# The pooling gate by seven products, with twelve quarter loads a stage and the differences made earlier

## The chip, the cores and the metric

One core of one Trainium2 chip. The time is the device time of one execution in microseconds (us); lower is better. The kernel before takes 1189.01 us, the median of three runs (1187.78 to 1189.39).

## What is computed

One decoder block on a sequence of 1024 tokens of width 1024, all in float32. The parts that matter here:

```python
h = rms_norm(x, norm_gain) * (1 + scale) + shift
q, k, v, z_a, u, z_b, m_a, m_b = split(h @ w_in)
p_a = (attention(q, k, v) * silu(z_a)) @ w_branch_a
pooled = multiscale_causal_pool(u, pool_w, pool_scale)   # windows 2, 4, 8, 16
p_b = (pooled * silu(z_b)) @ w_branch_b
out = (sigmoid(m_a) * p_a + sigmoid(m_b) * p_b) @ w_out
return rms_norm(x + gate * out, final_gain)              # gate from silu(c) @ w_ada
```

For each channel the pool takes the mean of the last 2, 4, 8 or 16 tokens minus the token itself: this is a *difference* below. There are eight of them, d_0 to d_7, each 128 channels by 1024 tokens, with windows 2, 2, 4, 4, 8, 8, 16, 16.

## The kernel before

**Products.** A float32 operand is held as a high half (rounded to the fast format float32r) and a low half (what is left of it). A product is three: high by high, high by low, low by high. ScalarE (ACT) casts the high half, VectorE (DVE) subtracts the low half. TensorE (PE) multiplies 128x128 by 128x512.

**Stages.** In order of time: the normalised input `h` and the projection u; the values v; the gate m_b (*m* below); the gate z_b of the pooling branch; the branch product with `w_branch_b` (*b* below); attention together with the other projections; the output. The stages v, m and b each multiply 1024x1024 by 1024x1024, cut into four blocks of 512 a side, with seven block products instead of eight (`seven`, L576). They differ in what is multiplied (`b_of`), what is loaded (`load`) and what is done with the results (`final`: `values`, `gate_b` and `branch`).

**A set.** A block product, called p1 to p7, is a set of 48 matmuls of PE in two quarters of 24. For each quarter `a_op` (L557) makes an operand from weights, in the tag `whl` with two buffers, and `b_op` (L563) one from the input, where the block product wants a sum of input blocks (p5, p6, p7, p4; the sums of h are in `ht0` to `ht3`, made by `make_t` during u). p1, p2 and p3 of v and m read h itself. The sets run in the order p1, p5, p6, p7, p4, p3, p2. Weight blocks are loaded in quarters, 512 KB each, 18 loads a stage: blocks that are needed in several sums are loaded again. `s2k` holds a sum of weights that p6 and p3 share. The results of a set stand in four banks (columns) of PSUM; they are copied by ACT or added by DVE (`copied`, `added`) and then given to `final`.

**The gate stage.** For each of eight blocks of 128 channels the loop makes the difference (`load_u` from the stored u, `make_d`), runs a projection of 48 matmuls (`project`, line name wzb), takes silu on ACT, and multiplies by the difference and the scale on DVE (L739). Sums of these, `t1` and `t2`, are made for b (L743 to L746). Beside it a row of `w_gate` is loaded and multiplied by silu(c) with a running sum (L752), which gives the final gate.

**Order.** In these stages a scheduler orders each engine's instructions by priorities that follow the program's order; every engine then runs its own queue in order, and an instruction that waits holds up all behind it on its engine. `tc.keep_in_program_order` pins an instruction to its written place. Loads are issued by SyncE (SP) and, for the stores of u, by ACT. Tiles of pools that have been closed give their space to later pools, so a later tile's first writer waits for the last use of the earlier one.

Of the kernel before, what the change touches and what calls it, by code (L numbers as in the profile page):

```python
# [15 lines left out]
P = 128  # L16
D = 1024
# [34 lines left out]
def block_kernel(ctx, tc, a, out):  # L52
# [28 lines left out]
    u_d = dram.tile([KB, P, S], F32, name="u_d")  # L81

# [8 lines left out]
    const.tile([P, 24], F32, name="skip")  # L91
# [440 lines left out]
    dhls = {}  # L532

    def load_u(j):
        u = dif.tile([P, S + 16], F32, tag="u", bufs=2, name=f"u{j}")
        v.memset(u[:, S:], 0.0)
        nc.sync.dma_start(u[:, :S], u_d[j])
        return u

    def make_d(j, u):  # L540
        win = WINDOWS[j // 2]
        cur, n, step = u, S + 16, 1
        while step < win:
            nxt = dif.tile([P, S + 16], F32, tag="win", bufs=2, name=f"win{j}_{step}")
            n -= step
            v.tensor_add(nxt[:, :n], cur[:, :n], cur[:, step:step + n])
            cur, step = nxt, 2 * step
        t0 = S - win + 1
        d = dif.tile([P, S], F32, tag="d", bufs=5, name=f"d{j}")
# [4 lines left out]
        dhls[j] = d  # L554
# [21 lines left out]
    def seven(nm, sums, load, b_of, a_moves, ta, tb, final, direct):  # L576
# [3 lines left out]
        def raw(first, m, k, q, name):  # L580
            t = (wts if first else sums).tile([P, 2, 512], F32, tag="raw" if first else "ar", bufs=2, name=f"{nm}{name}_{q}")
            load(t, m, k, q)
            return t

        def a_s1(q):
            r, w = raw(1, 1, 0, q, "a21"), raw(0, 1, 1, q, "a22")
            v.tensor_add(r, r, w)
            w = raw(0, 0, 0, q, "a11s")
            v.tensor_sub(k2(s2k, q), r, w)
            return r  # L590

        def a_s3(q):
            r, w = raw(1, 0, 0, q, "a11d"), raw(0, 1, 0, q, "a21d")
            v.tensor_sub(r, r, w)
            return r

        def a_s4(q):
            r = raw(1, 0, 1, q, "a12s")
# [4 lines left out]
            p1=lambda q: raw(1, 0, 0, q, "a11"), p5=a_s1, p6=lambda q: k2(s2k, q), p7=a_s3,  # L603
            p4=lambda q: raw(1, 1, 1, q, "a22"), p3=a_s4, p2=lambda q: raw(1, 0, 1, q, "a12"),
# [8 lines left out]
        for name in ("p1", "p5", "p6", "p7", "p4", "p3", "p2"):  # L613
            c = {"p5": "b", "p3": "b", "p2": "c"}.get(name, "a")
            if c not in chain:
                chain[c] = [bank((tb if c == "b" else ta)[j // 2], f"{nm}{name}_{j}") for j in range(4)]
            ps = chain[c]
            for q in range(2):
                al, bl = a_op(a_of[name](q), f"{nm}{name}a{q}"), b_of(name, q)
                for j in range(4):  # L620
                    js = slice(j * P, j * P + P)
                    for e in range(2):
                        for i, (w, m) in enumerate(((0, 0), (0, 1), (1, 0))):
                            l, r = (bl(m, e)[:, js], al[:, w, e]) if a_moves else (al[:, w, e, js], bl(m, e))
                            mm(
                                ps[j], l, r, start=name in ("p1", "p5", "p2") and (q, e, i) == (0, 0, 0),
                                stop=(q, e, i) == (1, 1, 2), skip_group_check=True,
                            )
            for j in range(4):
                if name == "p1":  # L630
                    keep["s1", j] = copied("s1", 4, j, ps[j])
                elif name == "p6":
                    keep["s2", j] = copied("s2", 4, j, ps[j])
                elif name == "p7":
                    final(1, 1, j, added(copied("s3", 4, j, ps[j]), chain["b"][j]))
                elif name == "p4":
                    final(1, 0, j, ps[j] if direct else copied("s3", 4, j + 4, ps[j]))
                elif name == "p3":
                    final(0, 1, j, added(keep["s2", j], ps[j]))
                elif name == "p2":  # L640
                    final(0, 0, j, added(keep["s1", j], ps[j]))

    with ExitStack() as vps:
# [3 lines left out]
        tq = [vp.tile([P, 4, 512], F32, name=f"ht{i}") for i in range(4)]  # L647

# [4 lines left out]
        def difference(dst, x, y, name):  # L653
            tmp = vp.tile([P, 2, 512], F32, tag="tmp", bufs=1, name=name)
# [24 lines left out]
        early.close()  # L679

        vs = vps.enter_context(pool("vs", side="right"))

        def h_parts(nm):
            def of(name, q):
# [3 lines left out]
                return b_op(k2(tq[("p5", "p6", "p7", "p4").index(name)], q), vs, 2, f"{nm}{name}b{q}")  # L688
# [7 lines left out]
        def values(m, n, j, src):  # L696
            sb = 4 * n + j
            vo = vs.tile([P, 8, 2, HD], F32R, tag="vo", bufs=3, name=f"vo{sb}_{m}")
# [6 lines left out]
            )  # L705

        def gate_b(m, n, j, src):
            t = vs.tile([P, 512], F32, tag="go", bufs=3, name=f"sb{4 * m + j}_{n}")
# [3 lines left out]
        seven("v", vs, loads("w_v"), h_parts("v"), True, ("av", "tr"), ("pj", "z"), values, True)  # L712
        seven("m", vs, loads("w_mb"), h_parts("m"), False, ("pj", "z"), ("av", "tr"), gate_b, True)

    turns[0] = cycle(("av", "tr", "pj", "z"))
    diffs = ExitStack()
    dif = diffs.enter_context(pool("dif", side="right"))

    pbs = ExitStack()
    pb = pbs.enter_context(pool("pb"))  # L720
    gb = pb.tile([P, KB, S], F32, name="gb")
    t1 = pb.tile([P, 4, 512], F32, name="t1")
    t2 = pb.tile([P, 4, 512], F32, name="t2")
# [499 lines left out]
```

## Time and profile before

| what | us |
|---|---|
| median of three runs | 1189.01 |
| the profiled execution | 1187.59 |
| its span, first to last instruction | 1185.8 |
| PE busy | 1169.2 |
| stage v | 128.5 to 204.6 |
| stage m | 204.6 to 280.8 |
| gate stage | 280.8 to 367.8 |
| stage b | 367.8 to 444.5 |

The granted TensorE clock is 0.998 of full speed in the mean. In the rows below, PE is TensorE, DVE VectorE, ACT ScalarE, POOL GpSimd, SP SyncE; a q behind the name is the engine's queue of DMAs. A row of a view by time has start, duration, engine, line, operation, output<-input, size and, in brackets, how long the engine was idle before it and what ended that. A row of groups has total busy time and mean nanoseconds, then idle time ahead. A row by tile has min/median/max nanoseconds and the first and last start. A row of DMA issues has the count, the size and the median time from issue to landing.

### The profile page before, as it was taken

How to read it: one execution, taken by the hardware profiler on the slowest of the kernel's cores; microseconds unless marked ns; L12 is line 12 of the kernel's file. 1: busy time of each engine (PE TensorE's matmuls, PEld its weight loads, DVE VectorE, ACT ScalarE, POOL GpSimd, SP SyncE). 2: the span in 40 equal slices, each digit the busy share in tenths (PEclk: the TensorE clock that was granted, in tenths of full speed). 3: DMA queues.
4: the chain of work that ended last, by engine and by line, in shares of the span. 5: the costliest groups of instructions: out<-in, count | busy, mean ns of one | idle time of the engine just before them, and what ended most of it. 6: DMA issues, size and time to landing. Idle time of an engine off the chain costs nothing.

```text
span 1185.8 us, 15373 instructions
## 1 busy us (share of the span) xinstructions
PE 1169.2 (99%) x5602; PEld 975.0 (82%) x5602; DVE 832.4 (70%) x1072; ACT 588.3 (50%) x1137; POOL 216.7 (18%) x248
## 2 busy tenths in 40 slices
PE   8999999999999999999999999999999999999997
PEld 7888888888888887888888888887888888888876
DVE  5767467555996651878788788879787973894653
ACT  5561355454313532667666666666666764232111
POOL 1000000000000004124234242443343622000001
PEclk9999999999999999999999999999999999999999
DMA  9651529546535257322333142423333126984622
GB/s 349 257 193 62 180 103 318 187 162 234 200 103 176 97 179 222 79 81 91 84 98 90 62 121 54 135 62 103 94 88 99 37 72 208 349 280 157 213 70 73
DMA packets 74750, 172.49 MB, mean 145 GB/s; under 512 B 9393, under 2 KB 22833, under 8 KB 72498
## 3 DMA queue, kind: packets, MB, share of 16 engines
q1 hardware_dynamic: 68770, 160.82, 41.6%
q10 hardware_dynamic: 5904, 10.68, 2.5%
q8 instruction: 44, 0.72, 0.3%
q14 instruction: 32, 0.26, 0.1%
HBM read 121.14 MB, written 33.56 MB: 130 GB/s over the span
## 4 chain that ended last, share of the span: by engine, by line
PE 84%; DVE 7%; DMA 3%; issue 3%; ACT 2%; SPq 0%; POOL 0%; POOLq 0%; DVEq 0%; ACTq 0%
PE p L101 24%; PE wzb L101 7%; PE mp L101 6%; PE vp L101 6%; PE bp L101 6%; PE o L101 6%; PE pa L101 5%; PE u L101 5%; PE z L101 5%; PE av L101 4%; PE wt L101 4%; PE ua L101 3%; DVE om L942 2%; DVE be L101 2%; PE wm L101 1%
## 5 line engine op out<-in xcount | busy, mean ns | idle before, releaser
L101 PE MATMUL p<-hT,w 128*128 128x512 f32 x1536 | 392.7, 392 | 1.3 <-DVE klo L101 1.3
L101 PEld LDWEIGHTS p<-hT,w 128*128 128x128 f32 x1536 | 283.0, 188 | 59.5 <-DVE klo L101 1.7
L942 DVE TENSOR_TENSOR_SCAN om<-om,eye 128x511 f32<-128x511 f32 (+7 forms) x128 | 184.0, 1442 | 68.9 <-ACT om L938 68.3
L149 POOL TENSOR_TENSOR w<-w_raw,w 128x256 fp32r<-128x256 f32 x124 | 124.8, 1037 | 571.5 <-ACT w L146 571.5
L938 ACT ACTIVATE om<-z 128x512 f32<-128x512 f32 (+2 forms) x192 | 95.0, 495 | 109.2 <-PE z L101 46.8
L962 DVE TENSOR_TENSOR wt<-wt,wt 128x512 fp32r<-128x512 f32 (+1 forms) x160 | 99.0, 619 | 15.7 <-ACT wt L961 14.7
L101 PE MATMUL av<-wt,vv 128*128 128x512 f32 x320 | 106.0, 412 | 0.1
L961 ACT CAST wt<-wt 128x512 fp32r<-128x512 f32 (+1 forms) x160 | 88.2, 551 | 35.0 <-PE wt L101 34.8
L101 DVE TENSOR_TENSOR be<-be,om 128x512 f32<-128x512 f32 (+7 forms) x128 | 98.5, 775 | 0.0
L101 PE MATMUL wt<-ident,be 128*128 128x128 f32 x576 | 90.3, 274 | 3.9 <-DVE wt L962 3.1
L939 ACT ACTIVATE be<-z 128x512 f32<-128x512 f32 (+2 forms) x192 | 94.0, 489 | 0.0
L101 PE MATMUL pa<-ga,wa 128*128 128x512 f32 x384 | 89.9, 390 | 0.9 <-DVE s L1115 0.8
L101 PE MATMUL o<-wo,mhl 128*128 128x512 f32 (+1 forms) x408 | 89.6, 377 | 0.0
L101 PE MATMUL wzb<-hT,wzb 128*128 128x512 f32 x384 | 87.2, 389 | 0.0
L101 PEld LDWEIGHTS pa<-ga,wa 128*128 128x128 f32 x384 | 71.9, 188 | 16.5 <-issue 1.2
L101 PEld LDWEIGHTS o<-wo,mhl 128*128 128x128 f32 x408 | 73.5, 188 | 14.1
L101 PEld LDWEIGHTS wt<-ident,be 128*128 128x128 f32 x576 | 69.5, 140 | 18.7 <-DVE wt L962 6.2
L101 PEld LDWEIGHTS wzb<-hT,wzb 128*128 128x128 f32 x384 | 72.1, 188 | 15.0
L991 POOL TENSOR_TENSOR tp<-tp,tl 128x256 f32<-128x256 f32 x32 | 38.1, 1190 | 153.9 <-DVE tp L988 153.9
L101 PE MATMUL z<-kl,q 128*128 128x512 f32 (+2 forms) x192 | 65.5, 341 | 0.0
L101 PE MATMUL z<-kh,q 128*128 128x512 f32 (+2 forms) x192 | 64.1, 334 | 0.0
L101 PE MATMUL u<-hT,wg 128*128 128x512 f32 x240 | 55.5, 391 | 0.0
(265 smaller groups left out, 1650.0 us busy)
## 6 DMA issues: line engine op xcount, KB each, us to landing
w_raw<-in_w_in SPq DMA_DIRECT2D x32, 512.0 KB, 3.5
v_d<-vo SPq DMA_DIRECT2D x16, 512.0 KB, 4.2
vv<-v_d SPq DMA_DIRECT2D x8, 1024.0 KB, 6.3
wa_raw<-in_w_branch_a SPq DMA_DIRECT2D x16, 512.0 KB, 4.7
wa<-in_w_mod SPq DMA_DIRECT2D x7, 1024.0 KB, 7.4
kh<-kh SPq DMA_DIRECT2D x48, 128.0 KB, 2.3
va<-in_w_v SPq DMA_DIRECT2D x10, 512.0 KB, 4.0
ma<-in_w_mb SPq DMA_DIRECT2D x10, 512.0 KB, 4.4
```

The lines of the kernel that those rows point to most:

```text
L101: ins = op(*args, **kw)
L149: gp.tensor_tensor(hl[:, 1, es], raw[:, es], hl[:, 0, es].bitcast(F32), op=ALU.subtract)
L938: act.activation(om[:, 1 + b0:1 + b0 + n], zp[:, :n], AF.Sigmoid, scale=-0.125)
L939: act.activation(be[:, b0:b0 + n], zp[:, :n], AF.Sigmoid, scale=0.125)
L942: v.tensor_tensor_scan(om[:, 1:W], om[:, 1:W], eye[:, :W - 1], 0.0, ALU.mult, ALU.max)
L961: act.copy(wt[:, 0, :off], pt[:, :off])
L962: v.tensor_sub(wt[:, 1, :off], pt[:, :off], wt[:, 0, :off].bitcast(F32))
L991: gp.tensor_add(tp, tp, tl)
```

## The change

The gate stage becomes a fourth `seven`, named z, in place of eight projections: 336 matmuls instead of 384. Its results go to `gate_z`, which loads the stored difference (`ds`, three buffers) for each column. All four stages get the new form of `seven`: the sets run in the order p1, p2, p6, p7, p5, p4, p3; block 11 of the weights is kept in tiles of its own (`a11`, in the new pool `vb`) and block 22 too, so that a stage makes 12 quarter loads instead of 18; in each quarter the high by high products of the first three columns (two in the second quarter) come first, and then the rest, column by column.

The differences are made during v and m: `paced` gives, for each set, what is done behind it ("load" j begins the load of u_j or of a row, "use" j makes the difference or multiplies the row; a name with "-" is done ahead of the set's results). They are stored in DRAM (`d_d`) and loaded again in z. The loads are begun by GpSimd's queue: `begin` lets GpSimd read one column of a result that has just been made (the mark), and issues the DMA behind it. The rows of `w_gate` go the same way in z and b. The first VectorE operation of each use is pinned.

```diff
+    def begin(dst, src, mark):
+        gp.tensor_scalar(spare[:, :1], mark[:, :1], 1.0, 0.0, op0=ALU.mult, op1=ALU.add)
+        tc.keep_in_program_order(gp.dma_start(dst, src))
...
-        nc.sync.dma_start(u[:, :S], u_d[j])
+        begin(u[:, :S], u_d[j], mark)
...
-            v.tensor_add(nxt[:, :n], cur[:, :n], cur[:, step:step + n])
+            ins = v.tensor_add(nxt[:, :n], cur[:, :n], cur[:, step:step + n])
+            if step == 1:
+                tc.keep_in_program_order(ins)
...
-        dhls[j] = d
+        gp.dma_start(d_d[j], d)
...
+        def a_s2(q):
+            r = raw("raw", 1, 0, q, "a21")
+            v.tensor_sub(a11[q], a11[q], r)
+            a22[q] = raw("a22", 1, 1, q, "a22")
+            v.tensor_sub(k2(s2k, q), a22[q], a11[q])
+            return k2(s2k, q)
...
-        for name in ("p1", "p5", "p6", "p7", "p4", "p3", "p2"):
+        for name in ("p1", "p2", "p6", "p7", "p5", "p4", "p3"):
...
+                ahead = 3 - q
+                parts_ = [(j, e, 0, 0) for j in range(ahead) for e in range(2)]
                 for j in range(4):
+                    for e in range(2):
+                        parts_ += [(j, e, w, m) for w, m in ((0, 0), (0, 1), (1, 0))[j < ahead:]]
...
-                return b_op(k2(tq[("p5", "p6", "p7", "p4").index(name)], q), vs, 2, f"{nm}{name}b{q}")
+                return b_op(k2(tq[("p5", "p6", "p7", "p4").index(name)], q), vb, 2, f"{nm}{name}b{q}")
...
-            nc.sync.dma_start(sb_d[4 * m + j][:, 512 * n:512 * n + 512], t)
+            act.dma_start(sb_d[4 * m + j][:, 512 * n:512 * n + 512], t)
...
+        pooled = paced(load_u, make_d, (
+            ("v", "p2", [("load", 3)]), ("v", "p6", [("use", 3), ("load", 0)]), ("v", "p7", [("load", 2)]), ("v", "p5-", [("use", 0)]),
+            ("v", "p5", [("load", 1)]), ("v", "p4", [("use", 2), ("load", 5)]), ("v", "p3", [("use", 1), ("load", 7)]),
+            ("m", "p1", [("use", 5), ("load", 6)]), ("m", "p6", [("use", 7), ("load", 4)]), ("m", "p5-", [("use", 6)]), ("m", "p4", [("use", 4)]),
+        ))
...
+        def modulated(j, wg_):
+            tc.keep_in_program_order(
+                v.scalar_tensor_tensor(wg_, wg_, 1.0, sg, ALU.mult, ALU.mult, accum_out=gate[:, j:j + 1]))
...
+            def gate_z(m, n, j, src):
+                ct = 4 * m + j
+                ds = zg.tile([P, 512], F32, tag="ds", bufs=3, name=f"ds{ct}_{n}")
+                gp.dma_start(ds, d_d[ct][:, 512 * n:512 * n + 512])
+                z = gq[m, n][:, j]
+                act.activation(z, src, AF.Silu)
+                v.scalar_tensor_tensor(z, ds, psc_v[:, ct:ct + 1], z, ALU.mult, ALU.mult)
+                return z
...
         def load_v(p):
-            nc.sync.dma_start(pair[p]["vv"].rearrange("p b h i d -> p (b h i d)").bitcast(F32), v_d[p].rearrange("p b c -> p (b c)"))
+            tc.keep_in_program_order(
+                nc.sync.dma_start(pair[p]["vv"].rearrange("p b h i d -> p (b h i d)").bitcast(F32), v_d[p].rearrange("p b c -> p (b c)")))
```

In b, the sums of the gated values are no longer made ahead: `g_parts` makes them on VectorE when p6, p5 and p4 ask for them, in `ht3` (for t1), `t2` and, for p5, in the block itself.

The change moves instructions in each queue. Three places follow. In a row, a name is the tile, with what it is read from behind the arrow; the brackets name the semaphores that it waits for (a name that ends in HW is a DMA of SP or ACT, in SW one of GpSimd).

**ACT, from the end of u to p1 of v.** `u0_sg1` is the last piece of u on its way to DRAM; `vp5b`, `vp6b` are b operands and `vp1a` weights of v. Before, with p1's weights cast long ahead:

```order
L185 COPY u0_sg1_1079<-u0_1_1054 128x512 [waits DMAHW2_49,PE_49]
L186 DMA u_d_78<-u0_sg1_1079 128x512 [waits Activation_49]
L565 CAST vp5b0_1174<-ht0_832 128x1024 [waits DVE_49]
L565 CAST vp5b1_1212<-ht0_832 128x1024 [waits DVE_49]
L609 COPY vs1_0_1151<-vp1_0_1089 128x512 [waits PE_49]
```

And after:

```order
L186 COPY u0_sg1_1083<-u0_1_1058 128x512 [waits DMAHW1_49,PE_49]
L187 DMA u_d_78<-u0_sg1_1083 128x512 [waits Activation_49]
L571 CAST vp6b0_1270<-ht1_834 128x1024 [waits DVE_49]
L571 CAST vp6b1_1306<-ht1_834 128x1024 [waits DMAHW3_49,DMAHW2_49,DVE_49]
L565 CAST vp1a0_1111<-va11_0_1109 128x1024 [waits DMAHW4_49]
L565 CAST vp1a1_1140<-va11_1_1138 128x1024 [waits DMAHW5_49]
L565 CAST vp2a0_1181<-va12_0_1179 128x1024 [waits DVE_49,PE_49]
```

The casts of p1's weights have moved behind the last piece of u and behind two casts for p6, of which the second waits for two DMAs: the last two stores of u, whose space its tile takes.

**VectorE in v, behind p2's results.** `vo2`, `vo3` are values on their way out, `win` and `d3` belong to difference 3, `vp7a`, `vp7b` are p7's operands. After:

```order
L733 TENSOR_TENSOR vo3_0_1253<-vs13_3_1173,vo3_0_1253 128x8x64 [waits Activation_49]
L550 TENSOR_TENSOR win3_1_1341<-u3_1257 128x1039 [waits DMASW0_49]
L566 TENSOR_TENSOR vp7a0_1355<-va11_0_1109,vp7a0_1355 128x1024 [waits Activation_49]
L550 TENSOR_TENSOR win3_2_1343<-win3_1_1341 128x1037 [waits DVE_49]
L572 TENSOR_TENSOR vp7b0_1358<-ht2_835,vp7b0_1358 128x1024 [waits Activation_49]
L556 SCALAR_TENSOR_TENSOR d3_1345<-win3_2_1343,u3_1257 128x1021 [waits DVE_49]
```

Before, no difference was made in this stage; p7's low halves followed p6's:

```order
L566 TENSOR_TENSOR vp6b1_1272<-ht1_833,vp6b1_1272 128x1024 [waits Activation_49]
L560 TENSOR_TENSOR vp7a0_1312<-va11d_0_1307,vp7a0_1312 128x1024 [waits Activation_49]
L566 TENSOR_TENSOR vp7b0_1315<-ht2_834,vp7b0_1315 128x1024 [waits Activation_49]
L560 TENSOR_TENSOR vp7a1_1347<-va11d_1_1342,vp7a1_1347 128x1024 [waits PE_49,Activation_49]
L566 TENSOR_TENSOR vp7b1_1350<-ht2_834,vp7b1_1350 128x1024 [waits Activation_49]
```

What is new there is the first window addition, which waits for a DMA of GpSimd and has p7's low halves behind it.

**ACT in b, at p5's second quarter.** `bs13` are copies of p7's results, `bp5a`, `bp4a` weights, `bp5b`, `bp4b` b operands. After:

```order
L620 COPY bs13_7_3192<-bp1_3_2886 128x512 [waits DMAHW4_49,PE_49,Pool_49]
L565 CAST bp5a1_3238<-ba11s_1_3235 128x1024 [waits DVE_49,Activation_49]
L565 CAST bp4a0_3278<-ba22_0_3041 128x1024 [waits PE_49,Activation_49]
L571 CAST bp5b1_3242<-ht2_835 128x1024 [waits DVE_49]
L571 CAST bp4b0_3282<-t2_2881 128x1024 [waits DVE_49,Activation_49]
```

Before, at the same product:

```order
L565 CAST p5b1_2955<-t1_2199 128x1024 [waits PE_49]
L559 CAST bp5a0_2914<-ba21_0_2906 128x1024 [waits DVE_49,Activation_49]
L609 COPY bs1_0_2894<-bp1_0_2826 128x512 [waits DMAHW5_49,DMAHW7_49,DMAHW2_49,PE_49]
L609 COPY bs1_1_2896<-bp1_1_2827 128x512 [waits PE_49]
L609 COPY bs1_2_2898<-bp1_2_2828 128x512 [waits PE_49]
L609 COPY bs1_3_2900<-bp1_3_2829 128x512 [waits PE_49]
L559 CAST bp5a1_2952<-ba21_1_2944 128x1024 [waits DVE_49,Activation_49]
```

The cast of p5's second b operand stood ahead of its first quarter's weights; now it stands behind the cast of p4's first weights, which waits for PE: that tile takes the buffer of p5's first quarter's weights. Its low half stands, on VectorE, behind these:

```order
L566 TENSOR_TENSOR bp5a1_3238<-ba11s_1_3235,bp5a1_3238 128x1024 [waits PE_49,Activation_49]
L824 TENSOR_TENSOR ht2_835<-ht2_835,g00_2310 128x1024
L566 TENSOR_TENSOR bp4a0_3278<-ba22_0_3041,bp4a0_3278 128x1024 [waits Activation_49]
L826 TENSOR_TENSOR t2_2881<-ht1_834,t2_2881 128x1024
L611 TENSOR_TENSOR ba12s_1_3389<-ba12s_1_3389,bs2k_2882 128x1024 [waits DMAHW6_49,DVE_49]
L572 TENSOR_TENSOR bp5b1_3242<-ht2_835,bp5b1_3242 128x1024 [waits Activation_49]
```

Here p4's low half, p4's difference and p3's weights are ahead of it.

More of the change, by code (lines that the diff above doesn't have):

```diff
@@ new lines, in seven @@
+                ends = {j: i for i, (j, *_) in enumerate(parts_)}
+                begun = set()
+                for i, (j, e, w, m) in enumerate(parts_):
+                    js = slice(j * P, j * P + P)
+                    l, r = (bl(m, e)[:, js], al[:, w, e]) if a_moves else (al[:, w, e, js], bl(m, e))
+                    mm(
+                        ps[j], l, r, start=name in ("p1", "p5", "p2") and q == 0 and j not in begun,
+                        stop=q == 1 and ends[j] == i, skip_group_check=True,
+                    )
+                    begun.add(j)
@@ L638, in seven @@
                 elif name == "p3":
[L639 to L641 removed]
+                    mark = final(0, 1, j, added(keep["s2", j], ps[j]))
+            for do in beside.get(name, ()):
+                do(mark)
     with ExitStack() as vps:
@@ L713, in block_kernel @@
[L713 to L723, printed above, removed]
-    gate = pb.tile([P, KB], F32, name="gate")
-    bias = pb.tile([P, KB], F32, name="gbias")
@@ L774, in branch, with paced, first_, then @@
-    def branch(m, n, j, t):
-        nc.sync.dma_start(pb_d[4 * m + j][:, 512 * n:512 * n + 512], t)
-    seven("b", sums, load_b_w, g_parts, False, ("av", "tr"), ("pj", "z"), branch, False)
-    pbs.close()
+            act.dma_start(sb_d[4 * m + j][:, 512 * n:512 * n + 512], t)
+            return t
+        banks = ("av", "tr"), ("pj", "z")
+        def paced(load, use, where):
+            held, todo = {}, {}
+            def first_(j, mark):
+                held[j] = load(j, mark)
+            def then(j, mark):
+                use(j, held.pop(j))
+            for stage, name, js in where:
+                todo.setdefault((stage, name), []).extend(
+                    [(lambda mark, j=j: first_(j, mark)) if at_ == "load" else (lambda mark, j=j: then(j, mark)) for at_, j in js])
+            return lambda stage: {name: dos for (st, name), dos in todo.items() if st == stage}
@@ new lines, in block_kernel @@
+        pooled = paced(load_u, make_d, (
[3 rows of a table added]
+        ))
+        seven("v", vs, loads("w_v"), h_parts("v"), True, *banks, values, True, pooled("v"))
+        seven("m", vs, loads("w_mb"), h_parts("m"), False, *banks, gate_b, True, pooled("m"))
+        diffs.close()
+        gp_ = vps.enter_context(pool("gp_", side="right"))
+        gate = gp_.tile([P, KB], F32, name="gate")
+        bias = gp_.tile([P, KB], F32, name="gbias")
+        nc.sync.dma_start(bias, a["b_gate"])
+        act.activation(sg, sg, AF.Silu)
@@ new lines, in block_kernel @@
+        with pool("zg", side="right") as zg:
+            def gate_z(m, n, j, src):
[6 more added lines that the diff above has]
+                return z
+            seven("z", vs, loads("w_zb"), h_parts("z"), False, *banks, gate_z, True, rows("z"))
```

148 lines of the change are left out of this document (73 added, 75 removed), and 4 rows, old and new, of the table rows.

## The prediction

> **What bounds the kernel now.** I read the page's busy shares, its chain, then busy time by stretches of the span and the stages' groups.
>
> ```profile
> PE 1169.2 (99%) x5602; PEld 975.0 (82%) x5602; DVE 832.4 (70%) x1072; ACT 588.3 (50%) x1137; POOL 216.7 (18%) x248
> PE   8999999999999999999999999999999999999997
> PE 84%; DVE 7%; DMA 3%; issue 3%; ACT 2%; SPq 0%; POOL 0%; POOLq 0%; DVEq 0%; ACTq 0%
> core 0: us, PE busy (x) PEld busy (x) DVE busy (x) ACT busy (x) POOL busy (x), PEclk, DMA share, GB/s
> 128.50:204.60 76.10, 76.10 (x337) 63.03 (x336) 51.30 (x55) 38.02 (x50) 0.00 (x0) 1.00 0.64 217
> 204.60:280.80 76.20, 76.20 (x338) 63.08 (x337) 43.30 (x44) 36.30 (x49) 0.00 (x0) 1.00 0.53 180
> 280.80:367.80 87.00, 87.00 (x385) 72.06 (x384) 73.17 (x107) 22.91 (x31) 0.00 (x0) 1.00 0.52 170
> 367.80:444.50 76.70, 76.70 (x336) 62.92 (x335) 49.20 (x48) 34.78 (x43) 2.84 (x4) 1.00 0.45 155
> 444.50:480.00 35.50, 34.24 (x151) 28.03 (x150) 8.20 (x9) 11.37 (x20) 13.13 (x19) 1.00 0.67 199
> ```
>
> PE is busy for 99% of the span and never idle in the four stages v, m, gate, b (76.1, 76.2, 87.0, 76.7 us of themselves); the clock is 1.00. So a removed product is worth its full pitch, and any operand that is late costs its full lateness: there is no slack on PE to lose it in. VectorE has room in v, m and b (51.3, 43.3, 49.2 us busy) and little in the gate stage (73.2 of 87.0).
>
> **What the change removes.**
>
> ```profile
> L101 PE MATMUL wzb<-hT,wzb x384: 389/389/389, 281.0 to 367.8; 128*128 128x512 f32 x192
> L101 PE MATMUL vp<-vp1a,hT x48: 389/389/389, 128.7 to 139.3; 128*128 128x512 f32 x48
> L609 ACT COPY bs<-bp 128x512 f32<-128x512 f32 x16 | 9.4, 587 | 6.9 <-PE bp L101 6.9
> ```
>
> 384 products start over 86.8 us: 0.2266 us each. Seven sets of 48 are 336, so 48 go: **−10.9 us**. Nothing else leaves PE. A set takes 48 × 0.2266 = 10.9 us, a quarter 5.4, and a quarter's first pass of hi·hi products covers 6 products (1.36 us) in a set's first quarter, 4 (0.91 us) in its second. That is the time for which a low half may lag its high half without cost.
>
> **Where VectorE's work goes.**
>
> ```profile
> L546 DVE TENSOR_TENSOR win<-u 128x1039 f32<-128x1039 f32 x8 | 9.9, 1235 | 5.5 <-DMA u<-u_d 5.5
> L752 DVE SCALAR_TENSOR_TENSOR wg<-wg,sg 128x1024 f32<-128x1024 f32 x8 | 9.8, 1221 | 0.6 <-DMA wg<-in_w_gate 0.5
> L739 DVE SCALAR_TENSOR_TENSOR gb<-d,vecs,gb 128x512 f32<-128x512 f32 x16 | 11.9, 746 | 7.5 <-ACT gb L738 7.5
> L550 DVE SCALAR_TENSOR_TENSOR d<-win,u 128x1021 f32<-128x1021 f32 x2 | 2.4, 1222 | 0.0
> ```
>
> Differences 3, 0, 2, 1 are made in v: 6 window additions of 1.235 and 4 scalings of 1.222, 12.3 us, so 51.3 becomes 64 of 76. Differences 5, 7, 6, 4 in m: 14 additions and 4 scalings, 22.2 us, 43.3 becomes 66. The new gate stage is m's 43.3, 16 scalings (11.9) and four modulation rows (4.9): 60. b gets six more 1024-wide subtractions (7.3) and four rows (4.9): 61. Every stage fits, so the sum is not bound by VectorE's total; it is bound by the order in which its work stands, since a pinned operation that waits holds up the low halves behind it. I walked the four stages along the new order with these durations.
>
> **The start of v.**
>
> ```profile
> 128.69 5.60 PE L101 MATMUL vp<-vp1a,hT 128*128 128x512 f32 x24
> 128.89 0.59 ACT L185 COPY u_sg<-u 128x512 f32<-128x512 f32 x1 [4.85 <-PE u L101]
> 129.50 0.33 ACTq L186 DMA_DIRECT2D u_d<-u_sg  x1
> L559 ACT CAST vp1a<-va x2: 1052/1054/1055, 71.2 to 81.4; 128x1024 fp32r<-128x1024 f32 x2
> u_d<-u_sg ACTq DMA_DIRECT2D x16, 256.0 KB, 2.0
> ```
>
> Before, p1's weights were cast at 71 and 81 us, so PE went on at once. After, ACT's queue has ahead of them two casts for p6, and the second waits for the landing of the last two stores of u, because its tile takes their space. The last copy starts at 128.89 as now, its store is issued at 129.50 and lands 2.0 later, 131.5; then two casts of 1.05 (or 0.96 at their pitch) and signals: PE restarts at about 133.8. **+5.1 us.** The low half follows one subtraction later, inside the 1.36 us of cover. For less, the store would have to land sooner; the bounds are 4.5 and 6.5.
>
> **v, behind p6.**
>
> ```profile
> u<-u_d SPq DMA_DIRECT2D x8, 512.0 KB, 4.7
> x<-in_x SPq DMA_DIRECT2D x8, 512.0 KB, 6.5
> wa<-in_w_mod SPq DMA_DIRECT2D x2, 512.0 KB, 10.0
> L235 POOL TENSOR_TENSOR st<-st,mhalf x8: 547/554/899, 12.5 to 67.1; 128x1 f32<-128x1 f32 x8
> ```
>
> u3's load begins after the last cast of p2's values (a GpSimd operation first, near 0.55 us by the nearest row), and its window addition is the first thing on VectorE ahead of p7's low halves. From that cast to p7's seventh product, window addition, low half, second addition and low half take 4.7 us, which leaves the load 3.7 us from mark to landing of the 8 to 9 that lie between that cast and p7's seventh product. No row shows a load on GpSimd's queue. The same load on SP took 4.7, and 512 KB took between 3.5 and 10.0 here: 4.7 stalls PE by 1.0, 6.5 by 2.7, 10.0 by 6. I take 5.5, since the mark adds to SP's 4.7: **+1.8 us**, ends 0 and 6.
>
> The row bounds this load from SP's side only. The Trainium skill, "DMA: Bandwidth & Descriptors", section "Anatomy of one DMA — SWDGE (gpsimd) path", fits 2.0 us plus bytes over 436e3 for a GpSimd DMA, an estimate of 3.2 us here, by which this term would be 0 and the sum 1.8 lower; no run here shows it.
>
> **m, gate and b.**
>
> ```profile
> ma12s<-in_w_mb SPq DMA_DIRECT2D x2, 512.0 KB, 4.4
> wg<-in_w_gate SPq DMA_DIRECT2D x8, 512.0 KB, 4.0
> 205.65 1.22 DVE L587 TENSOR_TENSOR ma<-ma,ma 128x1024 f32<-128x1024 f32 x1
> 206.78 0.68 DVE L573 TENSOR_TENSOR vs<-vp,vs 128x512 f32<-128x512 f32 x1
> 380.02 1.06 ACT L559 CAST bp5a<-ba 128x1024 fp32r<-128x1024 f32 x1 [0.19 <-DVE ba L587]
> 380.98 1.04 ACT L565 CAST p6b<-t 128x1024 fp32r<-128x1024 f32 x1
> ```
>
> Back to back, a 1024-wide subtraction takes 1.13 us and a cast 0.96. In m, p6's first low half ends about 1.3 us into p6 at best; behind it stand two additions and the scaling of difference 7, a sum of p2 (0.6) and the second quarter's operand with its low half: 1.3 + 0.6 + 5 × 1.13 = 7.6, due at 5.4 + 0.9 = 6.3. That is 1.3 late, and difference 5's row ahead adds about half an operation: **+1.9** (ends 1.3 and 3.3). Ahead of p4's low halves stand in m three additions of difference 6 and a subtraction that waits for a12's load (4.4 us), in the gate stage such a subtraction and a modulation row (4.0 on SP): each most of one operation late, **+0.9** and **+0.9** (ends 0 and 2). In b, p7 waits 0.4 behind row 4 (ends 0 and 2). **b's p5 is the second firm stall**: in ACT's queue the cast of p4's weights stands ahead of the cast of p5's second b operand, and it waits until PE has left p5's first quarter, whose weight tile it takes. So two casts (2 × 0.96, with signals 2.2) run after the quarter's end before PE can go on. It then has 0.91 us of hi·hi products, and the low half they lead to is the fourth of a row on VectorE that starts when p4's cast is done: p4's low half, p4's difference, p3's weights, p5's low half, 4 × 1.13 behind 1.1, ready 5.7 after the quarter's end. 5.7 − 0.91: **+4.8** (ends 2.2, the casts alone, and 6). p4 itself then finds its operands ready.
>
> **Start of attention.**
>
> ```profile
> 444.89 2.36 SPq L848 DMA_DIRECT2D vv<-v_d  x2
> 447.35 0.38 SPq L775 DMA_DIRECT2D pb_d<-bs  x1
> 455.96 1.07 ACT L833 CAST kh<-p 128x512 fp32r<-128x512 f32 x2 [9.64 <-DMA pb_d<-bs]
> 457.32 1.89 PE L101 MATMUL p<-hT,w 128*128 128x512 f32 x7 [1.26 <-DVE klo L101]
> ```
>
> The last store of b is stuck behind two loads of values, kh's cast waits for it, and PE idles 1.26. The loads move behind it: **−1.3**, ends 0 and −1.3. What follows has the same instructions on PE.
>
> **The sum**: −10.9 − 1.3 + 5.1 + 1.8 + 1.9 + 0.9 + 0.9 + 0.4 + 4.8 = +3.6 on the profiled execution's 1187.6 (its span 1185.8), and so on the median, 1189.0: **1192.6**. New work that I cost at nothing: GpSimd's marks and stores of differences (POOL is idle there), and the extra copies on ACT (0.59 each, half idle). If ACT had no slack beneath them, each copy would show with its 0.59.
>
> **Rivals.** *B, VectorE is never late.* What ACT's queue makes late is lost (start of v, and the two casts at b's p5), but loads land within 3.7 us and the hi·hi products cover the low halves: −10.9 − 1.3 + 5.1 + 2.2 = −4.9, **1184.1**, faster. It decides at 2.5 us: if VectorE's lateness, 8.5 us by my walk (1.8, 1.9, 0.9, 0.9, 0.4 and 2.6 of p5), stays under that in all, the change wins by over 0.2%. For it: five of the six terms are of a size that a load landing 2 us sooner removes. Against: the row ahead of p5's low half stands in the order itself.
> *C, loads on GpSimd's queue land late.* At 8 us for a load, v's p7 costs 2.5 more, m's p6 2, rows in the gate stage and b's p7 3, and gate_z, with four loads on three buffers, 2 to 3: **1202**. For it: 10.0 us for 512 KB occurs in this trace. Against: v's DMA share is 0.64, m's 0.53.
> The Trainium skill, "SBUF — State Buffer", section "SBUF: two separate sides", says that GpSimd writes the descriptors of its own DMAs and is locked out while VectorE runs a two-port copy, so such loads can starve; by that C is what happens where VectorE is busiest, but VectorE's operations in these stages are two-input ones and scalings, and no run here shows it.
> *D, the change does all that it says.* No stall shows, as ACT's casts and stores turn out not to hold each other: 1189.0 − 12.2 = **1177**. Against: both waits stand in the order.
>
> **How the numbers follow.** My sum, 1188 to 1197: 0.46 (0.17 of it under 1191.4). B, 1183 to 1188: 0.24 (0.15 of it under 1186.6). C, 1197 to 1206: 0.22. D: 0.08. A measurement of this kernel can tell about 0.2%, 2.4 us, from no change. So faster 0.15 + 0.08 = 0.23; same 0.17 + 0.09 = 0.26; slower 0.29 + 0.22 = 0.51. The range 1184 to 1202 leaves out D, the tail of C and little of B, under 0.2.
>
> **What would show it.** PE idle some 5 us before vp1's first product, named by ACT's cast behind the landing of u's stores; in b some 5 us lost at p5's second quarter; PE idle before p7 of v with VectorE's window addition waiting for u; the gate stage 10.9 us shorter in PE busy; no wait for klo at attention's start. The prediction is wrong if v starts without a gap, if p5's second quarter follows at once, or if loads on GpSimd land far from 5.5 us.

## The result, and the profile after

The changed kernel takes **1203.6 us**, the median of four runs (1202.49 to 1206.14), beside 1188.58 (1187.78 to 1189.39) for the kernel before on the same chip: a ratio of 1.0129, with a 95% interval of 1.0110 to 1.0149. It is slower by 15.0 us. The forecast was slower by 3.6, with 1202 as the upper end: the sign was right, the size was not, and the time lies 1.6 us above the range.

The page's busy shares of the changed kernel, its PE slices with the granted clock, and its chain:

```profile
PE 1163.9 (97%) x5554; PEld 967.2 (81%) x5554; DVE 862.1 (72%) x1100; ACT 613.0 (51%) x1165; POOL 253.4 (21%) x305
PE   8999899999999988999999999999999999999997
PEclk9999899999999999999999999999999999999999
PE 77%; DVE 10%; DMA 5%; issue 3%; ACT 3%; SPq 0%; POOL 0%; POOLq 0%; ACTq 0%; DVEq 0%
```

The 48 products are gone (5602 to 5554), but busy time fell by 5.3 only, and PE's share from 99% to 97%. The fifth slice (120 to 150 us) is less full and its clock below 9 tenths, and the fifteenth and sixteenth (420 to 480) are less full; PE's part of the chain fell from 84% to 77%, and that of VectorE, DMA and ACT together rose from 12% to 18%. Work was removed and waits came in.

PE's timeline of the changed kernel gives the waits one by one (start, duration, operation, then in brackets the idle time before it and what ended that):

```profile
132.53 13.61 PE L102 MATMUL vp<-vp1a,hT 128*128 128x512 f32 x48 [4.82 <-ACT vp1a L565]
170.67 9.81 PE L102 MATMUL vp<-vp7a,vp7b 128*128 128x512 f32 x42 [1.41 <-DVE vp7b L572]
236.97 2.79 PE L102 MATMUL mp<-mp6b,mp6a 128*128 128x512 f32 x11 [2.08 <-ACT mp6a L565]
241.04 3.26 PE L102 MATMUL mp<-mp6b,mp6a 128*128 128x512 f32 x13 [1.28 <-DVE mp6a L566]
245.04 5.86 PE L102 MATMUL mp<-mp6b,mp6a 128*128 128x512 f32 x24 [0.75 <-ACT mp6a L565]
422.04 1.66 PE L102 MATMUL bp<-bp5b,bp5a 128*128 128x512 f32 x6 [2.14 <-ACT bp5b L571]
424.61 1.89 PE L102 MATMUL bp<-bp4b,bp4a 128*128 128x512 f32 x7 [0.92 <-ACT bp4b L571]
435.31 5.73 PE L102 MATMUL bp<-bp4b,bp4a 128*128 128x512 f32 x24 [0.87 <-ACT bp4b L571]
469.31 5.78 PE L102 MATMUL p<-hT,w 128*128 128x512 f32 x24 [1.06 <-DVE klo L102]
477.47 3.72 PE L102 MATMUL p<-hT,w 128*128 128x512 f32 x15 [2.38 <-DVE qlo L102]
483.95 0.47 PE L102 MATMUL z<-kh,q 128*128 128x512 f32 x1 [2.76 <-DMA q<-qlo]
```

The four large stalls of the prediction (v's start, v's p7, m's p6, b's p5) are there by place. Of the small ones, those at m's p4 and b's p7 are not, and the gate stage's p4 shows only as 11.38 instead of 11.04; b's p4, which was to find its operands ready, waits. Two things are new: the first row's 48 products last 13.61, where a set without a wait lasts 11.04, and the last three rows, at attention's start, where the prediction had a gain.

The starts of the stages on PE in both profiled executions (1187.59 and 1202.49 us) turn this into an account. The first two columns are starts, in us; the third is what the stage that ends there became longer or shorter by, and the last what the prediction's terms for it come to:

| up to the start of | before | after | stage's change | predicted |
|---|---|---|---|---|
| v | 128.69 | 132.53 | +3.8 | +5.1 |
| m | 204.85 | 212.97 | +4.3 | +1.8 |
| the gate stage | 281.01 | 294.26 | +5.1 | +2.8 |
| b | 368.05 | 370.78 | −10.5 | −10.0 |
| attention | 444.97 | 451.76 | +4.1 | +5.2 |
| the first scores (z) | 471.75 | 483.95 | +5.4 | −1.3 |
| the end of the span | 1185.8 | 1200.7 | +2.7 | 0 |

### The profile page after: what moved, and what is told of

Read it like the earlier page. It is cut to its first block, busy times and chain, and to the rows that moved or that the text cites. A ratio compares the mean times of both kernels' runs of the same rounds, so it can differ in the third digit from the quotient of the medians.

```text
span 1200.7 us, 15400 instructions
## 1 busy us (share of the span) xinstructions
PE 1163.9 (97%) x5554; PEld 967.2 (81%) x5554; DVE 862.1 (72%) x1100; ACT 613.0 (51%) x1165; POOL 253.4 (21%) x305
## 4 chain that ended last, share of the span: by engine, by line
PE 77%; DVE 10%; DMA 5%; issue 3%; ACT 3%; SPq 0%; POOL 0%; POOLq 0%; ACTq 0%; DVEq 0%
PE p L102 23%; PE pa L102 7%; PE zp L102 6%; PE o L102 6%; PE bp L102 6%; PE u L102 5%; PE z L102 4%; PE av L102 4%; PE wt L102 4%; PE mp L102 4%; PE ua L102 3%; DVE om L1000 2%; PE vp L102 2%; DVE be L102 2%; DMA kh<-kh 1%
## 5 line engine op out<-in xcount | busy, mean ns | idle before, releaser
L102 PEld LDWEIGHTS u<-hT,wg 128*128 128x128 f32 x240 | 44.8, 188 | 9.6 <-issue 0.5
L102 PEld LDWEIGHTS av<-wt,vv 128*128 128x128 f32 x320 | 48.5, 191 | 0.6 <-DVE wt L1020 0.5
```

What stands on the lines that cost most here:

```text
L102: ins = op(*args, **kw)
```

## The experiments

Each edit is made in the changed kernel, so each time is compared with 1203.6, unless another kernel is named. The kernel before was run beside each and took 1187.6 to 1188.6; the ratio in brackets is to it. Rows of a timeline are those of one execution, and the runs of one kernel lie 2 to 6 us apart, so a gain of 4 us needs its place in the rows beside it. In the edits' lines, a name like `vp1a0` is p1's first quarter of weights in v.

**The start of v: where the gap comes from.** The first edit loads p1's weights of v into the ordinary weight tiles, which are free early, beside the kept ones.

```diff
+            first = raw("raw", 0, 0, q, "a11f") if nm == "v" else None
             a11[q] = raw("a11", 0, 0, q, "a11")
-            return a11[q]
+            return first or a11[q]
```

> The changed kernel, but p1 of v reads weights of its own, loaded into the tile that p1 used before the change, so that they can be cast during u; block 11 is loaded once more. Theory: the gap of 4.8 us ahead of p1 of v and the slow clock behind it (p1 took 13.5 us instead of 10.9) are one cost with one cause, the cast behind the landing of u's last stores. Both go: 1203.6 less 4.8 less 2.6 is 1196.2. Rival: the slow clock has nothing to do with the gap and stays: 1198.8.

Measured: **1193.13** (1192.15 to 1197.11; ratio 1.0047, 1.0031 to 1.0064), 10.5 less. PE's timeline of this kernel at the start of v:

```profile
125.81 2.88 PE L102 MATMUL u<-hT,wg 128*128 128x512 f32 x12
128.53 11.04 PE L102 MATMUL vp<-vp1a,hT 128*128 128x512 f32 x48
```

No gap, and p1 takes 11.04 again. So the casts' place behind u's stores was the cause. The stall at v's p7 is gone too, and VectorE's timeline of this kernel says why: with the added load, p7's low half stands ahead of the window addition that it stood behind.

```profile
158.20 1.22 DVE L572 TENSOR_TENSOR vp7b<-ht,vp7b 128x1024 fp32r<-128x1024 f32 x1
160.53 1.24 DVE L550 TENSOR_TENSOR win<-u 128x1039 f32<-128x1039 f32 x1 [1.11 <-DMA u<-u_d]
```

So the edit changed more than the start. Up to m's start PE is 8.3 us ahead of the changed kernel: 4.0 at v's start, 2.6 of clock in p1 and 1.7 at p7. The late start cost more than its 4.82, but not all of the 10.5. The rest doesn't show in this execution, the slowest of its five (1197.11): m, b, attention's start and what follows it were each 0.5 to 1.0 longer in it than in the changed kernel.

The second edit leaves the loads and pins ACT's casts, so that p1's two stand ahead of p6's.

```diff
-        act.copy(hl[:, 0], src)
+        ins = act.copy(hl[:, 0], src)
+        if name in ('vp1a0', 'vp1a1'):
+            tc.keep_in_program_order(ins)
...
+        if name in ('vp6b0', 'vp6b1'):
+            tc.keep_in_program_order(ins)
```

> The changed kernel, but ACT's casts of p1's weights in v are pinned ahead of the two casts for p6, so that only u's last copy stands ahead of them. Theory: PE's gap shrinks from 4.8 to some 2.2 us, and a gap that short does not bring the slow clock: p1 takes 10.9 us, the time is 1203.6 less 5.2, 1198.4. Rival: any gap brings the slow clock: only 2.6 us are gained, 1201.0.

Measured: **1204.45** (1203.04 to 1205.21; 1.0135, 1.0120 to 1.0150): no gain. PE's timeline:

```profile
130.26 11.22 PE L102 MATMUL vp<-vp1a,hT 128*128 128x512 f32 x48 [2.12 <-ACT vp1a L565]
166.97 11.65 PE L102 MATMUL vp<-vp7a,vp7b 128*128 128x512 f32 x44 [2.83 <-DVE vp7b L574]
```

The gap shrank to 2.12 and p1 ran at full clock, as meant; but p7 waited 2.83 instead of 1.41, and its 44 products then took 11.65 (10.27 for the same 44 in the kernel with all corrections, below). Of the gain at v's start (2.7 of gap, 2.4 of clock, less 0.4 because u ended later here) p7 took back 3.0. The rest went in b and at attention's start: a wait of 0.74 came at b's p7, and behind waits of nearly the same length as in the changed kernel the products were slower: six of b's p5 took 2.51 instead of 1.66, and 15 at attention's start 5.30 instead of 3.72. So p1's stall moved on in part to the next late operand; the other part is not shown to come from the edit.

**Does the gap slow the clock?** The granted clock of the changed kernel in stretches of 2 us (PE busy, products, clock, DMA share, GB/s):

```profile
132.00:134.00 2.00, 1.47 (x4) 0.50 0.00 0
134.00:136.00 2.00, 2.00 (x6) 0.50 0.00 0
136.00:138.00 2.00, 2.00 (x6) 0.56 0.00 0
138.00:140.00 2.00, 2.00 (x10) 1.00 0.00 0
```

Six products in 2 us instead of nine to ten, at a clock of 0.50 to 0.56, for some 5 us behind the gap: that is p1's 2.6. To tell the gap from its place, 20 products that nothing reads fill it.

```diff
+        filler = bank("pj", "filler")
+        for _ in range(20):
+            mm(filler, hT[:, 0, 0, :P], hT[:, 0, 0, :512], start=True, stop=True)
```

> The changed kernel with 20 more products on PE, of h by h into a bank of PSUM that nobody reads, between the last of u and the first of v. At their pitch of 0.2266 us they take 4.5 us, about the whole gap of 4.82 in which PE waits for p1's weights; the data come as late as before. Theory 'the gap slows the clock': PE is busy up to p1, the clock reads 1.00 there, p1 takes 10.9 us instead of 13.46, and the time is 1203.6 - 2.6 = 1201.0. Rival 'the slow clock is another matter' (it comes at this place whatever PE did before): p1 still takes 13.4, and the time is 1203.6.

Measured: **1199.55** (1198.62 to 1203.45; 1.0109, 1.0092 to 1.0126). PE's timeline:

```profile
128.65 4.70 PE L102 MATMUL filler<-hT 128*128 128x512 f32 x20
133.62 11.22 PE L102 MATMUL vp<-vp1a,hT 128*128 128x512 f32 x48 [0.28 <-ACT vp1a L565]
```

The clock of the same kernel in the first 2 us of p1:

```profile
134.00:136.00 2.00, 2.00 (x10) 1.00 0.00 0
```

The weights came as late as before (4.8 behind u's end in both) and p1 took 11.22 at a clock of 1.00. The idle time itself brings the slow clock at this place; that is shown. (The time fell by 4.1, not by 2.6, and its interval overlaps that of the changed kernel. In this execution m was 1.3 shorter, with a wait of 0.82 instead of 2.08 at p6, and what follows attention's start 1.7 shorter, while attention's start was 0.9 longer; none of this is shown to come from the edit.)

**The gate's store at the start of attention.** In the changed kernel the final gate is written to memory at 456.48 instead of 343, as 1024 pieces of 4 bytes. DMA issues of the changed kernel from 455 to 470 (count, size, median us to landing):

```profile
kl<-klo SPq DMA_DIRECT2D x2, 128.0 KB, 8.6
g_d<-gate POOLq DMA_DIRECT2D x1, 4.0 KB, 11.2
```

Those of the kernel before, at the same place in attention (448 to 466):

```profile
kl<-klo SPq DMA_DIRECT2D x4, 128.0 KB, 2.3
```

And in its gate stage (340 to 356):

```profile
g_d<-gate SPq DMA_DIRECT2D x1, 4.0 KB, 11.7
```

The store took as long before (11.7), but in the gate stage, where nobody waited. Now the first keys' low halves are moved beside it and take 8.6 instead of 2.3. A load of weights, 512 KB at 456.56, runs beside them too, so these rows alone do not name the store. The edit stores the gate in rows of 32 bytes, and turns it into its order in memory in the middle of attention.

```diff
-        gp.dma_start(g_d[0].rearrange("(k p) -> p k", p=P), gate)
+        gp.dma_start(gp_d, gate)
...
+                if p * 8 + k == 8:
+                    tc.keep_in_program_order(gp.dma_start(g_d[0].rearrange("(k p) -> p k", p=P), gp_d))
```

> The changed kernel, but the final gate is stored at the same place by the same queue in 128 rows of 32 bytes, and turned into its 1024 single numbers by a DMA later in attention. Theory: the store of 1024 pieces of 4 bytes (11.2 us) beside the first loads of k's halves holds them back, and the gaps of 1.1, 2.4 and 2.8 us at attention's start come from it; they go, 1197.4. Rival: they come from b's last stores and from GpSimd's queue as such: the gaps stay, 1203.6.

Measured: **1197.63** (1196.06 to 1198.16; 1.0076, 1.0061 to 1.0091), 6.0 less. DMA issues of this kernel from 450 to 470:

```profile
gp_d<-gate POOLq DMA_DIRECT2D x1, 4.0 KB, 3.8
```

The moves of the first keys' high halves stand at the same place in both kernels, 1.5 us behind the store. First in the changed kernel (458 to 461), then in this one (458 to 461):

```profile
kh<-kh SPq DMA_DIRECT2D x2, 128.0 KB, 9.7
```

```profile
kh<-kh SPq DMA_DIRECT2D x2, 128.0 KB, 2.8
```

PE's waits for klo and qlo are gone, and 1.26 are left before the first scores, for q's low half. From attention's start to the first scores it is 26.6 us, beside 32.2 in the changed kernel and 26.8 in the kernel before. The store's 4-byte pieces are the cause of attention's loss, 5.6 us. But the 1.3 that were to be won there did not come without it either: the wait for klo went, and the one for q's low half came in its place.

**p5 of b.** One edit pins the casts and low halves of p5's and p4's operands in their written places.

```diff
+    PINNED, PINNED_LOW = ('bp5b1', 'bp4a0', 'bp4b0', 'bp4a1', 'bp4b1'), ('bp5b1', 'bp4b0')
```

> The changed kernel, but in b the casts of p5's second operand and of p4's operands are pinned in the order of the products, and their low halves too. Theory: p5's stall of 2.1 and 0.9 us falls to about 1.3 (the difference on VectorE still ends at the quarter's end); p4 loses about 0.5 to its low half, behind the sums of p5: a gain of some 3 us of the 4.8, 1200.6. Rival: the order on ACT is not the cause, VectorE's backlog is, and the stall moves on to p4 at the same size: 1203.6.

Measured: **1203.38** (1199.3 to 1205.51; 1.0133, 1.0115 to 1.0151). The wait at p5 fell from 2.14 to 0.98, but at p4 1.19 and 0.49 stand instead of 0.92 and 0.87; b was 1.2 shorter. The median shows no gain, and its four runs spread by 6 us: what this edit is worth in time stays open. The other one keeps these pins and also makes the differences of gated values for p5 and p4 earlier, with p7's operands.

```diff
-            elif name == "p5":
+            elif name == "p7":
...
-            elif name == "p4":
```

> As the run with p5's and p4's casts pinned in b, and the two differences that p5 and p4 need are made a product earlier, at p7. Theory: b's stalls (4.8 us in the changed kernel) need both: the order on ACT and the differences in time; with both, b runs with under 0.5 us lost and the time is 1203.6 less 4.4, 1199.2. Rival: VectorE is simply full in b, and the subtractions that come earlier push p7's low halves late by as much: 1203.6.

Measured: **1199.79** (1197.59 to 1201.15; 1.0101, 1.0086 to 1.0116), 3.8 less, and b runs without a wait, as PE's timeline shows:

```profile
415.07 11.04 PE L102 MATMUL bp<-bp5b,bp5a 128*128 128x512 f32 x48
425.95 11.04 PE L102 MATMUL bp<-bp4b,bp4a 128*128 128x512 f32 x48
436.83 11.04 PE L102 MATMUL bp<-bp3b,bp3a 128*128 128x512 f32 x48
```

The sets follow each other at 10.88, and b takes 76.5, beside 81.0 in the changed kernel. There the walk's row on VectorE stood as foreseen: p4's low half, p4's difference and p3's weights ran between the end of p5's first quarter (419.90) and p5's low half, which ended 5.8 us behind it.

```profile
421.07 1.23 DVE L566 TENSOR_TENSOR bp4a<-ba,bp4a 128x1024 fp32r<-128x1024 f32 x1 [1.38 <-ACT bp4a L565]
...
424.48 1.22 DVE L572 TENSOR_TENSOR bp5b<-ht,bp5b 128x1024 fp32r<-128x1024 f32 x1
```

The pins alone gave 1.2 of b's 4.5, both together all of it. The differences moved without the pins were not run, so what each is worth by itself stays open.

**p6 of m.** GpSimd's timeline of the changed kernel at the start of m:

```profile
208.78 0.18 POOL L535 TENSOR_SCALAR spare<-vo 128x1 f32<-128x1 f32 x1 [11.88 <-ACT vo L732]
218.33 0.59 POOL L560 DMA_DIRECT2D d_d<-d  x1 [9.37 <-DVE d L559]
219.19 0.54 POOL L536 DMA_DIRECT2D u<-u_d  x1 [0.27 <-issue]
```

VectorE's timeline, the addition that waits for that load:

```profile
226.13 1.24 DVE L550 TENSOR_TENSOR win<-u 128x1039 f32<-128x1039 f32 x1 [2.26 <-DMA u<-u_d]
```

The mark for u5 is made at 208.78, the load starts at 219.19: `u` has two buffers, the load wants that of u2, and difference 2 still reads it until 218, where its store also stands ahead in GpSimd's queue. VectorE then waits 2.26 with m's p6 behind. The edit gives `u` a third buffer, and the window sums too (the room comes from writing a difference over its last window sum).

```diff
-        u = dif.tile([P, S + 16], F32, tag="u", bufs=2, name=f"u{j}")
+        u = dif.tile([P, S + 16], F32, tag="u", bufs=3, name=f"u{j}")
...
-        d = dif.tile([P, S], F32, tag="d", bufs=2, name=f"d{j}")
+        d = cur[:, :S]
```

> The changed kernel, but u's rows have three buffers, and a difference is written over its last window sum, so that the space is the same. Theory: u5's load is issued 10 us after its mark, since its buffer is that of u2, and the window addition of difference 5 waits 2.3 us for it; without that p6 of m loses 5.1 less 2.3 us: 1201.3. Rival: VectorE's row of work in m alone makes p6 late, and nothing changes: 1203.6.

Measured: **1199.14** (1197.3 to 1202.67; 1.0101, 1.0083 to 1.0120), 4.5 less. Of m's 4.1 us of waits 1.32 are left: u5's load now starts 0.8 us behind its mark (205.75 and 206.55), VectorE no longer waits for it, and m is 3.5 shorter. The buffer was the cause of the larger part. The stall at v's p7 is gone too, as in the first edit because its low half now stands ahead of the window addition (165.01 and 167.80); that is 1.5 of the 4.5.

**The middle of attention.** The pinned load of values now stands right ahead of the next keys. SP's queue of the changed kernel:

```profile
775.10 0.42 SPq L906 DMA_DIRECT2D vv<-v_d  x1
775.62 1.14 SPq L873 DMA_DIRECT2D kl<-klo  x2
```

In the kernel before it was issued well ahead of them:

```profile
746.47 0.38 SPq L848 DMA_DIRECT2D vv<-v_d  x1
...
762.86 1.10 SPq L816 DMA_DIRECT2D kl<-klo  x2
```

The two moves behind the 1 MB load took 7.5 to landing, beside 4.7 before, and PE waited 1.87 for transposed weights. PE's timeline there:

```profile
785.11 0.66 PE L102 MATMUL wt<-ident,be 128*128 128x128 f32 x4 [1.87 <-DVE wt L1020]
```

The granted clock behind it (third number from the right):

```profile
786.00:788.00 2.00, 2.00 (x7) 0.57 0.40 86
```

The edit calls that load at the keys' step, one step earlier.

```diff
-                pair[p] = dict(kh=tile_("kh", [2, S]), kl=klz[p % 2])
+                pair[p] = dict(kh=tile_("kh", [2, S]), kl=klz[p % 2], vv=tile_("vv", [8, 2, 2, HD], pl=at))
...
-                if use is use_za:
+                if use is (use_k if p > 1 else use_za):
```

> The changed kernel, but from the third pair of heads on the load of values is pinned ahead of k's moves of the same pair, not behind them. Theory: the pin of this load puts 1 MB right ahead of a move of k's low half, which then takes 7.5 us instead of 4.7, and PE's gap of 1.9 us at 785 us and the slow clock behind it (1.7 us) come from that; both go: 1203.6 less 3.6, 1200.0. Rival: the gap has another cause; 1203.6.

Measured: **1202.96** (1201.89 to 1204.54; 1.0131, 1.0116 to 1.0146). The wait at 785 and the slow clock behind it are gone, and the moves took 4.7 again, but the median fell by 0.6 only: within what the runs spread. The gain shows in the stage. The same wait stands, at 1.57 to 2.16, in the profiled executions of the changed kernel and of the seven kernels above without this edit, and from the first scores to the end they take 715.1 to 717.8; this kernel and the three below, which keep the edit, have no such wait and take 713.1 to 713.4 (714.1 before). So it is worth 2 to 4 us there. In this execution v's start, b and attention's start were 0.6 to 1.5 longer than in the changed kernel, which hides it; why they were is open.

**All corrections together:** early weights, gate in rows, differences behind p7 with the pins, three buffers for u, values one step earlier.

> All of these together: early weights for p1 of v, the gate stored in rows, casts pinned and differences earlier in b, values loaded ahead of k's moves, three buffers for u. Theory: the costs are apart and add: 1203.6 less 10.5 (early weights, measured), 6.0 (gate, measured), 4.4, 3.6 and 2.3 is 1176.8, faster than the kernel before by 1%. Rival: they overlap, VectorE's lateness that one of them hid shows when it goes, as with the pinned cast in v: 1182 to 1186.

Measured: **1180.75** (1179.54 to 1181.43; 0.9941, 0.9924 to 0.9957): 22.9 below the changed kernel (the five gains measured singly add up to 25.4) and 0.6% below the kernel before, between what the theory and the rival had. m takes 80.8 in it, nearly as in the changed kernel (81.3), in spite of the three buffers. PE's waits in v and m that were left:

```profile
162.67 10.27 PE L103 MATMUL vp<-vp7a,vp7b 128*128 128x512 f32 x44 [1.03 <-DVE vp7b L577]
227.91 2.79 PE L103 MATMUL mp<-mp6b,mp6a 128*128 128x512 f32 x11 [0.58 <-ACT mp6a L568]
232.57 10.28 PE L103 MATMUL mp<-mp6b,mp6a 128*128 128x512 f32 x37 [1.87 <-DVE mp6a L571]
```

**VectorE's order, taken further.** To that kernel, differences 3 and 7 one set later, with the low halves of p7 (v) and p6 (m) pinned. Of the lines the parts that change:

```diff
-            ("v", "p6", [("use", 3), ("load", 0)]), ("v", "p7", [("load", 2)]),
+            ("v", "p6", [("load", 0)]), ("v", "p7", [("use", 3), ("load", 2)]),
...
-            ("m", "p6", [("use", 7), ("load", 4)]),
+            ("m", "p6", [("load", 4)]), ("m", "p7", [("use", 7)]),
```

> The kernel with all the corrections (1180.75), with the differences 3 and 7 made one set later (behind p7 instead of p6) and the low halves of p6 in m and of p7 in v pinned, so that no window addition stands ahead of them. Left of stalls there are 1.03 at p7 of v and 0.58 + 1.87 at p6 of m, with slow clock behind the latter. Theory 'VectorE's order is all that is left': both go, with the slow clock behind them, some 3.5 us and what the clock adds (about 1.5): 1176. Rival 'the work only moves': the additions then hold up p5 or p4 of m, whose operands stand behind them, and the time stays at 1180 to 1181.

Measured: **1185.03** (1183.43 to 1187.25; 0.9978, 0.9969 to 0.9988), 4.3 slower than without. One row of PE's timeline says why:

```profile
254.07 12.54 PE L103 MATMUL mp<-mp5b,mp5a 128*128 128x512 f32 x48 [6.42 <-ACT mp5a L568]
```

Both waits went, and a new one of 6.42 came, with 1.5 of slow clock behind it: difference 7 and the first window addition of difference 6 now stood together ahead of p5's weights (240.7 to 251.7 on VectorE). The rival had the mechanism right, but not the size: it said 1180 to 1181. So the last kernel makes them behind those operands:

```diff
-            ("m", "p7", [("use", 7)]), ("m", "p5-", [("use", 6)]), ("m", "p4", [("use", 4)]),
+            ("m", "p5-", [("use", 7)]), ("m", "p5", [("use", 6)]), ("m", "p3", [("use", 4)]),
```

> As the run before (1185.03), but in m the differences 7, 6 and 4 are made behind the operands of p5, behind p5 and behind p3, so that no window addition stands ahead of p5's weights, which PE waited 6.42 for in that run. Theory 'each stall was the row on VectorE ahead of the operand': p6 stays without a stall and p5 loses its own, with the 1.5 of slow clock behind it; beside the 1180.75 of the kernel with all the corrections, 1.03 + 0.58 + 1.87 of stalls and some 1.5 of clock are gone: 1175 to 1177. Rival 'the work only moves on': difference 4, now made at the start of the gate stage, holds up p1, p2 or p6 there or the loads of differences, and the time is 1180 or more.

Measured: **1175.78** (1175.23 to 1177.68; 0.9898, 0.9880 to 0.9916), 1.0% faster than the kernel before, and within the 1175 to 1177 of the theory. Its busy shares:

```profile
PE 1157.5 (99%) x5554; PEld 965.3 (82%) x5554; DVE 862.2 (73%) x1100; ACT 612.7 (52%) x1165; POOL 249.7 (21%) x306
```

All waits of PE between 100 and 520 in its timeline:

```profile
342.38 4.39 PE L103 MATMUL zp<-zp4b,zp4a 128*128 128x512 f32 x18 [0.38 <-DVE zp4b L579]
460.32 0.47 PE L103 MATMUL z<-kh,q 128*128 128x512 f32 x1 [1.03 <-DMA q<-qlo]
```

VectorE, ACT and GpSimd are as busy as in the changed kernel (862.1, 613.0, 253.4); PE's waits are gone but for 0.38 and 1.03. That is the time of the prediction's rival D (1177), which took the change without its stalls: the 27.8 us between the two kernels are order, buffers, one store and p1's weights of v loaded a second time.

## Why the prediction was right in places and wrong in size

**Right, place and size.** The product count: the gate stage lost 10.5 in all, of 10.9 less 0.9 foreseen. The gap at v's start: 4.82 for 5.1, by the mechanism named (casts behind the landing of u's stores). v's p7: 1.41 for 1.8, by the window addition ahead of p7's low half: where that order turned, in two kernels, the wait went. The size is in part luck: this load took 5.7 from issue and 6.4 from its mark, where 5.5 from the mark was taken, but p7's seventh product was due later too; in the other kernels with this order the wait was 1.0 to 2.8. b: 4.8 above seven sets of 10.88 for 5.2, by the casts and the row on VectorE that the walk named. That the total fits is in part luck too: PE ran seven products of p4 while p5 waited, and lost about 1 us at p4's second quarter, which was to lose none. The changed kernel's row of these loads:

```profile
u<-u_d POOLq DMA_DIRECT2D x8, 512.0 KB, 5.4
```

The Trainium skill, "DMA: Bandwidth & Descriptors", section "Anatomy of one DMA — SWDGE (gpsimd) path", whose fit gives an estimate of 3.2 for such a load, is not borne out by it.

**Wrong: "What follows has the same instructions on PE", and −1.3 for attention's start.** This step failed most: +5.4 came, 6.7 off. Of these the store's pieces are 5.6, as the run with the gate in rows shows; the other 1.1 are the gain that did not come even there, because q's low half was then awaited instead of klo. The text counted which instructions PE has and which loads leave SP's queue, but not that the gate's store moves too, from the gate stage to beside the first keys, and what its 4-byte pieces do to moves of 128 KB. The prediction followed the rows of modulation from stage to stage, but not to their end: the store's 11.7 us were in the trace of before, at 343, and were not looked up.

**Wrong: idle time priced at its own length.** Each stall was taken as the time that PE waits. At v's start the wait also cost 2.6 of slow clock, which filling the gap removed. At 786 to 790 the clock reads 0.57 for 4 us, some 1.7 lost by that reading, behind a wait of 1.87 that came from the pinned load of values, which the prediction had seen only as a gain. The time lies 1.6 above the range: without attention's store, or without the slow clock at v's start, it would have been inside.

**Right mechanism, wrong size: m's p6, +1.9.** With p4's 0.9 m was to lose 2.8, and lost 5.1, all at p6. The term was worked out from VectorE's operations in a row; that difference 5's load cannot begin before difference 2 has left its buffer, 10.4 us after its mark, is not in it. p4 of m lost nothing. Three buffers took most of the loss away in a kernel with nothing else changed.

**The rivals.** B falls: VectorE was late in v, m and b. C gave about the right time (1202) for a wrong reason: the u loads took 5.4 in the median (3.7 to 7.0), not 8, and the gate stage with its loads of differences lost only some 0.4. D describes what the change can do, not what it did.

The differences add up: 6.7 at attention's start, 2.6 of clock at v, 2.3 in m, 2.7 in the rest of attention, less 1.1 in b, 0.5 in the gate stage, 0.4 at v's gap and p7, and 1.0 because u ended earlier in this execution (at 127.7, where v began at 128.7 before), make 11.3; 3.6 + 11.3 = 14.9.

## What to carry to other kernels

Where PE has no slack, list for every step that moves not only its operations but the stores at its end, and look up what they cost where they stood: a transfer that was hidden is a price that waits. Add to each stall of a few us what the clock can lose behind it. And put early work behind the operands of the next product, not ahead of them: the last two kernels have the same instructions and took 1185.0 and 1175.8 us by the place of three differences alone. A small edit can also turn the order of instructions that it does not name, as at v's p7, so look at the rows before a gain is put down to it.

## What the runs showed of the hardware

The clock fell after some short idle times of PE and not after others. After waits of 1.41 and less no slow set is seen in the rows above. The gap of 4.82 at v's start and the one of 6.42 in m were always followed by a slow clock (the first in six kernels, where p1 took 12.71 to 13.80 instead of 11.04). In between it went both ways. In the changed kernel the clock read 1.00 behind the waits of 2.08 in m and of 2.38 and 2.76 at attention's start, but 0.57 behind the 1.87 at 785. At that place the wait was 1.87 in four kernels: two had the slow clock behind it (the changed one, and the one with p1's casts pinned, at 0.50), two had 1.00 (p5 pinned, and three buffers). The wait of 2.83 at v's p7 was followed by 0.50, and one of 3.05 at attention's start, with the differences earlier, by 1.00. At b's p5 the same wait of 2.14 left six products at 1.66 us in the changed kernel and made them 2.93 with the gate in rows. The Trainium skill, "TensorE: Matmul & The Clock Gate", section "Part 1: The HAM clock gate (the "warmup" mystery)", has the clock halved after an idle window of about 3.4 us and released after as long a busy one: the 0.50 agrees, the 5 us of slow clock at v's start are a little longer, and the waits of 1.87 and 2.83 show that less can be enough. What decides between 1.8 and 3.1 us stays open; the length alone does not, since 1.87 at the same place did both.

One 4 KB store in 4-byte pieces took 11.2 to 11.7 us to land, beside 3.8 for the same bytes in 32-byte rows, and behind it two moves of 128 KB on SP's queue took 9.7, beside 2.8 behind the 32-byte rows at the same place.
